# Mixers for one token tile and then for three, in a block of HGRN2, dilated attention and an expert layer

## The chip, the core and the metric

The kernel runs on one core of a Trainium2 chip. The metric is device microseconds of one execution. An engine takes its instructions one after the other, in the order in which the built program has them: TensorE (PE, with its weight loads as PEld), VectorE (DVE), ScalarE (ACT), GpSimd (POOL) and SyncE (SP, which only issues transfers).

## The reference, cut to what matters

512 tokens of width 1024 pass one layer. Everything is float32 outside, and comes out in float32.

```
h = RMSNorm(x);  [q,f,i,og | q,k,v | gate_a | gate_b] = h @ W_in
y_a = HGRN2(q,f,i,og)              # 4 heads, state 128x128 carried over chunks of 64 tokens
y_b = three dilated causal windows, one softmax
x   = x + (sigmoid(gate_a) * (y_a @ W_a) + sigmoid(gate_b) * (y_b @ W_b)) @ W_out
h2  = RMSNorm(x)
q   = h2 @ W_q;  per token and head: the top 16 of 128 x 128 key pairs  (8 heads -> 128 experts of 16384)
x   = x + sum over the 128 pairs of  gelu(u[e] . h2) * gate * v[e]
```

The tokens lie in four tiles of 128 (tile 0 to tile 3). A tile's state depends on the tiles before it, so tiles are mixed in order; the expert layer of a tile needs that tile alone.

## The kernel before, in words

**Mixers.** `Front` (L144) does the mixers of one half of the tokens, and the queries of their expert layer. It is called twice, for tiles 0 and 1 (L716), then for tiles 2 and 3 (L756). Each call streams all dense weights, 37 slots of 256 columns, in tiles `w` of four row blocks (`slot`, L180). The first half is "split": weights and activations are cut into a high and a low float32r half (`halves`, L93: ACT writes the high half, DVE or POOL the low one), and each product is done as three matmuls with 256 moving columns. The second half takes plain float32 matmuls, which the trace shows as two instructions each.

**Routing.** `routing` (L532) picks the 128 experts of every token of a tile, mostly on DVE, in many short instructions.

**The expert layer** reaches its rows in two ways. *Gathered*: for tiles 0 and 3 `u_steps` (L622) lets POOL gather one row of u per token, 128 times (`row`, L616, 512 KB a time), and a DVE pass (L626) takes its dot product with h2; `v_steps` (L637) does the same with v for tile 3 (pass L645). *Streamed*: `hidden` (L783) multiplies all of u, in 128 blocks, with h2 of tiles 1 and 2 (24 matmuls a block), and the last loop (L817) multiplies all of v, block by block, with the weights of tiles 1, 2 and 0 (18 matmuls a block, L834). The weights of a block come from `scatter_steps` (L659): for four tokens at a time DVE makes one-hot rows `e` (L666) and products `eg` (L670), PE multiplies them (L680), ACT stores the result, and it goes to DRAM as `g_d`, from which the last loop loads `Gc`. A block's product begins with the DVE multiplication L825.

**The order.** A scheduler puts each engine's instructions in an order when the program is built. The code guides it: `Pump` (L690) puts steps of gathering and scattering between other work, `ROWS_P` allows 99 gathered rows ahead of the second half's last norm, and L807 holds all but the other tile's gathered rows back:

```
807    with tc.issue_after(last_e2[0].ins):
808        rows(4)
```

Here the u rows of tile 3 are put behind the scatter step's last `eg`; the v rows are added behind them.

Of the kernel before, what the change touches and what calls it, by code (L numbers as in the profile page):

```python
# [22 lines left out]
HALF = 256  # L23
NT = HALF // P
# [13 lines left out]
# Token tiles by how the expert layer reaches them: rows of u gathered, u streamed whole, v streamed whole.  # L38
# VD starts with UD; the tile that is not in it gathers its rows of v.
# [4 lines left out]
NV = len(VD) * P  # L44
GT = 16
NGT = NV // GT
GB = 8
# the first weights' low halves are Pool's
LPOOL = 4
# steps of gathering and scattering before the end of the second half's mixers  # L50
ROWS_P, SCAT_PP = 99, 5
# blocks of hidden values ahead of the products with v, and places for them
NPRE, RING = 46, 58
# tokens in a group of the scatter, groups in flight; groups whose third part ACT scales
GS, EGB = 4, 2
ACT3 = {1: (0, 4, 8, 12), 0: (0, 4, 8, 12), 2: (0, 8)}
ROWS_F, ROWS_D, SCAT_F = 3, 2.0, 0.4
UK, WBUFS, ATB = 4, 4, 3

# columns of the packed per-partition parameters  # L60
C_G1, C_HGN, C_LB, C_QG, C_KG, C_END = 0, 8, 9, 17, 18, 19
# columns of the packed shape constants
M_ATT, M_HG, M_END = 0, 512, 640
# slots of the packed dense weights
# [4 lines left out]
def kernel(ctx: ExitStack, tc: tile.TileContext, x, wst, par, cst, cols, g2, keys, u, v, ut, vr, out):  # L69
# [9 lines left out]
    nc.scalar.activation(root, eps[:, 0:1], AF.Sqrt)  # L79
    h2g = {}  # L80
    hH = const.tile([P, KC, NU], F32R, name="hH")
    hL = const.tile([P, KC, NU], F32R, name="hL")

    fctx = ExitStack()
    wp = fctx.enter_context(tc.tile_pool(name="wp", bufs=WBUFS, side="right"))
    hp = fctx.enter_context(tc.tile_pool(name="hp", bufs=1, side="right"))
# [3 lines left out]
    psb = fctx.enter_context(tc.tile_pool(name="psb", bufs=2, space=PSUM, side="right"))  # L90
# [7 lines left out]
    def accumulate(out, ws, xs, cut, w_stays):  # L98
        """Sum over the blocks of w x, in three products where they come in two parts."""
        ops = []  # L100
        for k, w in enumerate(ws):
            if isinstance(w, tuple):
                x = xs[0][:, k], xs[1][:, k]
                ops += [(w[0], x[0]), (w[0], x[1]), (w[1], x[0])]
            else:
                ops.append((w, xs[:, k]))
        for i, (w, x) in enumerate(ops):
            l, r = (w[:, cut], x) if w_stays else (x[:, cut], w)
            nc.tensor.matmul(out, l, r, start=(i == 0), stop=(i == len(ops) - 1))  # L109
# [10 lines left out]
    reset = fp.tile([P, HALF], F32, name="reset")  # L120
# [3 lines left out]
    # lower bound: softmax over the two logit rows, row 0  # L124
# [5 lines left out]
    # values of the first group by token; of the other two with every fourth token's in a row  # L130
# [13 lines left out]
    class Front:  # L144
        """The mixers of one half of the tokens, and the queries of their expert layer."""

        def __init__(self, h, hi_pool, after_unit):
            self.h, self.hi_pool, self.after_unit = h, hi_pool, after_unit
            split = self.split = hi_pool is not None
            self.units = 0  # L150
            hT = hp.tile([P, KC, HALF], F32R if split else F32, name="hT")
            g1 = par_sb[:, C_G1:C_G1 + KC]
            for t in range(NT):
                xn = sp.tile([P, D], F32, name="sc")
                nc.sync.dma_start(out=xn, in_=x[h * HALF + t * P:h * HALF + (t + 1) * P])
# [3 lines left out]
                for c in range(0, KC, 4):  # L159
# [4 lines left out]
                    if split:  # L164
                        xg = sp.tile([P, 4, P], F32, name="pT")
                        nc.vector.tensor_mul(xg, pt, gain)
                        # the high half lies where h2 of the streamed tokens comes later
                        halves(hH[:, c:c + 4, tk], hT[:, c:c + 4, tk], xg)
                    else:
                        nc.vector.tensor_mul(hT[:, c:c + 4, tk], pt, gain)  # L170
            self.hT = (hH, hT) if split else hT
# [8 lines left out]
        def slot(self, i, ks=slice(0, KC)):  # L180
            """Row blocks ks of a slot's weights, UK of them in a tile: the blocks' operands in order."""
            ops = []
            for k0 in range(ks.start, ks.stop, UK):
                n = min(UK, ks.stop - k0)
                w = wp.tile([P, UK, 256], F32, name="w")
                load = nc.sync.dma_start(out=w[:, :n], in_=wst[i][:, k0 * 256:(k0 + n) * 256].rearrange("p (k c) -> p k c", k=n))
                self.after_unit(load)
                if self.split:
                    w = halves(self.hi_pool.tile([P, UK, 256], F32R, name="wh")[:, :n],
                               self.hi_pool.tile([P, UK, 256], F32R, name="wl")[:, :n], w[:, :n],  # L190
                               nc.gpsimd if self.units < LPOOL or self.units % 4 == 0 else nc.vector)
                self.units += 1
                ops += [tuple(a[:, k] for a in w) if self.split else w[:, k] for k in range(n)]
            return ops

        def proj(self, i, x, T):
            """A slot's 256 columns of the half's products with x, on the partitions (T) or along them."""
            w = self.slot(i)
            pt = psb.tile([P, 2, 256], F32, name="pp")
            for j in range(2):  # L200
                accumulate(pt[:, j], w, x, slice(j * P, (j + 1) * P), T)
            return pt

        def proj_T(self, i):
            return self.proj(i, self.hT, True)

        def proj_N(self, i):
            return self.proj(i, self.hT, False)

        def proj_hgrn(self):  # L210
            pa = hp.tile([P, 2, HG_HEADS, HALF], F32, name="pairA")
            pb = hp.tile([P, 2, HG_HEADS, HALF], F32, name="pairB")
            sq, kk, lf, G2 = pa[:, 0], pa[:, 1], pb[:, 0], pb[:, 1]
            vs = hp.tile([P, 2, NT, 512], F32, name="vs")
            self.vt, self.sil = vs[:, 0], vs[:, 1]
            for b in range(2):
                pt = self.proj_T(W_IN + b)
                nc.scalar.activation(sq[:, 2 * b:2 * b + 2], pt, AF.Sigmoid)
            for b in range(2):
                pt = self.proj_T(W_IN + 2 + b)  # L220
                nc.scalar.activation(lf[:, 2 * b:2 * b + 2], pt, AF.Sigmoid)
# [5 lines left out]
            shp = [P, HG_HEADS, HALF // CH, CH]  # L227
            G = G2.rearrange("p h (c s) -> p h c s", s=CH)
            for hd in range(HG_HEADS):
                nc.vector.tensor_tensor_scan(G2[:, hd], reset, lf[:, hd], 0.0, op0=ALU.mult, op1=ALU.add)  # L230
            eG = hp.tile(shp, F32, name="eG", tag="yaT")
            self.dec = sp.tile([P, HG_HEADS, HALF // CH], F32, name="dec")
            nc.scalar.activation(eG, G, AF.Exp)
            nc.vector.tensor_copy(self.dec, eG[:, :, :, CH - 1])
            nc.vector.tensor_tensor(out=lf.rearrange("p h (c s) -> p h c s", s=CH),
                                    in0=G[:, :, :, CH - 1:CH].to_broadcast(shp), in1=G, op=ALU.subtract)
            nc.scalar.activation(lf, lf, AF.Exp)
            nc.scalar.activation(G2, G2, AF.Exp, scale=-1.0)
            nc.vector.tensor_mul(sq, sq, eG.rearrange("p h c s -> p h (c s)"))
# [3 lines left out]
            for b in range(2):  # L243
                pt = self.proj_N(W_IN + 4 + b)
                nc.scalar.activation(self.vt[:, :, b * 256:(b + 1) * 256], pt, AF.Copy)
            for b in range(2):
                pt = self.proj_N(W_IN + 6 + b)
                o = self.sil[:, :, b * 256:(b + 1) * 256]
                nc.scalar.activation(o, pt, AF.Sigmoid)
                nc.vector.tensor_mul(o, pt, o)  # L250
            self.yaT = hp.tile([P, HG_HEADS, HALF], F32R if self.split else F32, name="yaT", tag="yaT")
            if self.split:
                self.yaT = self.yaT, self.hi_pool.tile([P, HG_HEADS, HALF], F32R, name="yaL", bufs=1)
# [56 lines left out]
        def proj_attn(self):  # L310
            h = self.h
            qgain, kgain = par_sb[:, C_QG:C_QG + 1], par_sb[:, C_KG:C_KG + 1]
            for b in range(3):
                pt = self.proj_N(W_IN + 14 + b).rearrange("p t (n e) -> p t n e", e=64)
                if b == 0:
                    nc.scalar.activation(va[:, h * NT:(h + 1) * NT], pt, AF.Copy)
                    continue
# [476 lines left out]
    with tc.tile_pool(name="php", bufs=2, space=PSUM, side="right") as php, \  # L794
# [6 lines left out]
        for b in range(NPRE):  # L801
            hidden(b, php)
# [100 lines left out]
```

## Time and profile before

| what | us |
|---|---|
| runs: median (lowest to highest of 3) | 1849.44 (1844.27 to 1850.57) |
| profiled execution: span | 1845.0 |
| PE busy | 1674.0 (91%) |
| DVE busy | 1444.1 (78%) |
| ACT busy | 795.6 (43%) |
| POOL busy | 793.6 (43%) |
| read from HBM, written | 443.85 MB, 28.84 MB |

The span of the profile is the time from the first to the last instruction of one execution; the runs have 4.4 us more in the median. A busy share is a mean over stages that have different limits, so a stage is read by itself: the mixers of the first half (0 to 285 us), those of the second (285 to 704), routing, scattering and the first blocks of hidden values (704 to 1055), and the loop of block products (1055 to 1845).

### The profile page before, as it was taken

What the parts mean: (1) busy time and instruction counts of PE and PEld (TensorE: products, weight loads), DVE (VectorE), ACT (ScalarE), POOL (GpSimd) and SP (SyncE); (2) the same over time, 40 slices, a digit from 0 to 9 for tenths busy, and PEclk for the clock granted to TensorE, in tenths of its full rate; (3) what the DMA queues carried; (4) which work ended last, traced back from release to release, by engine and by line L of the source; (5) the groups of instructions that cost most, each with busy time, mean ns of one, the idle gap of its engine ahead of it and who ended that gap; (6) DMA issues with size and microseconds to landing.
All of it is one profiled execution on the core that took longest, in us unless ns stands there. A gap on an engine that the chain in (4) does not pass through costs nothing.

```text
span 1845.0 us, 28370 instructions
## 1 busy us (share of the span) xinstructions
PE 1674.0 (91%) x10573; PEld 1482.8 (80%) x10573; DVE 1444.1 (78%) x2681; ACT 795.6 (43%) x1348; POOL 793.6 (43%) x546
## 2 busy tenths in 40 slices
PE   6999889889789989888867899999999999999987
PEld 6998888667667878777867878888888888888766
DVE  5644547887887758999999977877877788888777
ACT  5655551211114556368756534343343434343232
POOL 3211312463664335556566543344323464444442
PEclk9999999988899989889978899999999999999999
DMA  6453553778787887534455799999988999999887
GB/s 196 153 158 119 175 194 118 270 235 276 244 279 264 297 298 261 183 111 145 152 183 202 238 372 334 339 328 326 367 298 299 345 339 341 340 340 317 288 309 278
DMA packets 169963, 475.61 MB, mean 258 GB/s; under 512 B 14304, under 2 KB 62688, under 8 KB 168800
## 3 DMA queue, kind: packets, MB, share of 16 engines
q1 hardware_dynamic: 112416, 270.56, 43.0%
q0 software_dynamic: 55296, 201.35, 30.9%
q10 hardware_dynamic: 2112, 1.88, 0.3%
q8 instruction: 83, 1.36, 0.3%
q14 instruction: 56, 0.46, 0.1%
HBM read 443.85 MB, written 28.84 MB: 256 GB/s over the span
## 4 chain that ended last, share of the span: by engine, by line
PE 47%; DVE 25%; DMA 11%; issue 9%; POOL 5%; ACT 1%; DVEq 0%; POOLq 0%; SPq 0%; ACTq 0%
PE acc L834 19%; PE pp L109 13%; PE ph L109 10%; DMA row<-in_u_dram,idx 6%; DVE row L626 4%; DVE e L666 4%; DVE eg L670 3%; POOL row L618 3%; DMA Gc<-g_d 3%; PE pg L680 2%; PE pr L680 1%; DVE cs L564 1%; DVE rest L515 1%; DVE ti L514 1%; DVE h2g L645 1%
## 5 line engine op out<-in xcount | busy, mean ns | idle before, releaser
L618 POOL DMA_INDIRECT row<-in_u_dram,idx x206 | 254.9, 1237 | 383.8 <-DVE row L626 274.3
L626 DVE SCALAR_TENSOR_TENSOR row<-row,h2g 128x1024 f32<-128x1024 f32 x206 | 272.4, 1328 | 62.2 <-DMA row<-in_u_dram,idx 61.3
L109 PE MATMUL ph<-hH,uh 128*128 128x256 f32 x1024 | 302.1, 295 | 7.1 <-ACT pre L792 6.0
L109 PE MATMUL ph<-hH,ul 128*128 128x256 f32 x1024 | 302.9, 296 | 5.0 <-POOL ul L95 5.0
L109 PE MATMUL ph<-hL,uh 128*128 128x256 f32 x1024 | 299.0, 292 | 0.0
L834 PE MATMUL acc<-vl,ah 128*128 128x512 f32 x768 | 241.8, 396 | 9.3 <-DVE vl L95 9.3
L834 PE MATMUL acc<-vh,al 128*128 128x512 f32 x768 | 240.0, 393 | 0.0
L94 ACT ACTIVATE uh<-ub 128x1024 fp32r<-128x1024 f32 x128 | 136.7, 1068 | 230.7 <-PE ph L109 214.1
L834 PE MATMUL acc<-vh,ah 128*128 128x512 f32 x768 | 222.5, 395 | 9.9 <-ACT vh L94 9.9
L109 PEld LDWEIGHTS ph<-hH,uh 128*128 128x128 f32 x1024 | 205.9, 201 | 12.8 <-ACT pre L792 7.8
L109 PEld LDWEIGHTS ph<-hH,ul 128*128 128x128 f32 x1024 | 205.5, 201 | 6.3 <-POOL ul L95 5.8
L109 PEld LDWEIGHTS ph<-hL,uh 128*128 128x128 f32 x1024 | 204.6, 200 | 3.8
L680 PEld LDWEIGHTS <-e 128*128 128x128 bf16 x1152 | 124.8, 119 | 73.4 <-DVE eg L670 65.4
L834 PEld LDWEIGHTS acc<-vl,ah 128*128 128x128 f32 x768 | 143.2, 190 | 40.0 <-DVE vl L95 11.8
L834 PEld LDWEIGHTS acc<-vh,ah 128*128 128x128 f32 x768 | 142.9, 190 | 38.2 <-ACT vh L94 10.5
L834 PEld LDWEIGHTS acc<-vh,al 128*128 128x128 f32 x768 | 145.5, 190 | 31.8
L94 ACT ACTIVATE ah<-Gc 128x384 fp32r<-128x384 f32 x128 | 66.9, 523 | 229.4 <-PE acc L834 226.7
L95 DVE TENSOR_TENSOR vl<-vb,vh 128x1024 fp32r<-128x1024 f32 x128 | 156.1, 1219 | 12.2 <-ACT vh L94 12.0
L618 POOL DMA_INDIRECT row<-in_v_dram,idx x76 | 111.6, 1469 | 120.0 <-DVE h2g L645 109.2
L680 PE MATMUL pg<-eg,e 128*128 128x128 bf16 x768 | 103.1, 297 | 51.8 <-DVE eg L670 51.3
L94 ACT ACTIVATE vh<-vb 128x1024 fp32r<-128x1024 f32 x128 | 135.6, 1059 | 28.6 <-DMA vb<-in_vr_dram 27.9
L674 ACT ACTIVATE eg<-e,pk 128x128 bf16<-128x128 bf16 x320 | 115.4, 565 | 70.9 <-DVE e L666 68.1
(279 smaller groups left out, 3582.4 us busy)
## 6 DMA issues: line engine op xcount, KB each, us to landing
w<-in_wst_dram SPq DMA_DIRECT2D x140, 512.0 KB
ub<-in_ut_dram SPq DMA_DIRECT2D x128, 512.0 KB
vb<-in_vr_dram SPq DMA_DIRECT2D x128, 512.0 KB
Gc<-g_d SPq DMA_DIRECT2D x15, 1536.0 KB
g_d<-Gx SPq DMA_DIRECT2D x16, 960.0 KB
g_d<-Gx SPq DMA_DIRECT2D x8, 1024.0 KB
row<-in_u_dram,idx POOLq DMA_INDIRECT x206
sc<-in_x_dram SPq DMA_DIRECT2D x4, 512.0 KB
```

Of the source, the lines that this page charges most:

```text
L94: nc.scalar.activation(hi, x, AF.Copy)
L95: (eng or nc.vector).tensor_tensor(out=lo, in0=x, in1=hi.bitcast(F32), op=ALU.subtract)
L109: nc.tensor.matmul(out, l, r, start=(i == 0), stop=(i == len(ops) - 1))
L514: nc.vector.max_index(out=ids[:, 0:8], in_max=vals[:, 0:8], in_values=src)
L515: nc.vector.match_replace(out=rest[:, :w], in_to_replace=vals[:, 0:8], in_values=src, imm_value=-BIG)
L618: nc.gpsimd.indirect_dma_start(out=r, out_offset=None, in_=src, in_offset=bass.IndirectOffsetOnAxis(ap=index, axis=0))
L626: nc.vector.scalar_tensor_tensor(r, r, 1.0, h2g[T], op0=ALU.mult, op1=ALU.mult, accum_out=hid[:, g, j:j + 1])
L666: nc.vector.tensor_tensor(out=e12, in0=iota[:, None].to_broadcast([P, 2, NKEY, GS]), in1=e[:, 0:2].to_broadcast([P, 2, NKEY, GS]), op=ALU. ...
L670: last_e2[0] = nc.vector.tensor_tensor(out=eg[:, :n], in0=e12[:, 1:2].to_broadcast([P, n, NKEY, GS]), in1=e[:, 2:2 + n].to_broadcast([P, n ...
L674: nc.scalar.activation(eg[:, 2, :, q], e12[:, 1, :, q], AF.Copy, scale=pk3[:, VD.index(T), i + k + q:i + k + q + 1])
L680: nc.tensor.matmul(pt[:, q], e12[:, 0, :, q0 + q], eg[:, j, :, q0 + q], start=(j == 0), stop=(j == 2))
L834: nc.tensor.matmul(acc[t][c], lt, r[:, c * 512:(c + 1) * 512], start=(b == 0 and i == 0), stop=(b == NKEY - 1 and i == 2))
```

## The change

`Front` now takes a list of tiles: first tile 0 alone, with plain float32 matmuls of 128 moving columns, then tiles 1 to 3, split, with 384 moving columns (or 256 where the tokens are the stationary side). Tile 0 is no longer scattered. Its 128 weights are summed per expert on DVE (`same`, 128 passes of 128 elements) and each sum is written by POOL as 128 single words to `w_d` in DRAM, in eight groups of 16 writes, each group behind the one before it (`spread_steps`). The last loop loads `Wc` from there beside `Gc`. The gathering of tile 0's rows and these word writes are spread over the second call's weight loads (`ROWS_F`, `SPREAD_F`). Gathered rows have four places in place of three (before, tile 3's had two more). The routing of tiles 1 to 3 and the scatter steps of tiles 1 and 2 stand between the first 50 blocks of hidden values; the order rule of L807 is gone.

```diff
-UK, WBUFS, ATB = 4, 4, 3
+ROWS_F, SPREAD_F = 2.4, 3.6
+NPRE, RING = 50, 56
+LDVE = 3
+ROUTE1, ROUTE2, SCAT_H = 6, 22, 2
+ROWS_H, ROWS_D = 0.8, 1.8
+UK, WBUFS, WSBUFS, ATB = 4, 2, 4, 2
...
+    def spread_steps():
+        for j in range(P):
+            same = rt.tile([P, P], F32, name="same")
+            nc.vector.scalar_tensor_tensor(same, fulls, fulls[:, j:j + 1], hid[:, 0], op0=ALU.is_equal, op1=ALU.mult,
+                                           accum_out=wsum[:, j:j + 1])
+            d = nc.gpsimd.indirect_dma_start(out=w_d.rearrange("i j t -> (i j t)")[:, None], in_=wsum[:, j:j + 1],
+                                             out_offset=bass.IndirectOffsetOnAxis(ap=place[:, j:j + 1], axis=0),
+                                             in_offset=None)
...
+            if j % TOPK == 0:
+                before, spread[:] = list(spread), []
+            behind(d, before)
...
+    f = Front(UG[:1], False, lambda load: None)
...
+    f = Front(tuple(range(1, 4)), True, background)
...
     routing(0, rq0)
-    rows.add(u_steps(0))
...
+    rows.add(u_steps(UG[0]))
+    rows.add(spread_steps())
+    mixers(f)
...
-                     nc.gpsimd if b < NPRE else nc.vector)
+                     nc.gpsimd if b < NPRE and b % LDVE else nc.vector)
...
-        routing(2, rq2)
-        scat.add(scatter_steps(0, pg_bank))
-        scat.add(scatter_steps(2, pg_bank))
-        scat(P)
-        for b in range(NPRE):
-            hidden(b, php)
-        routing(3, rq3)
...
-    rows.add(u_steps(3))
-    with tc.issue_after(last_e2[0].ins):
-        rows(4)
+        routing(3, rq3)
+        rows.add(u_steps(3))
+        for b in range(NPRE):
+            if b == ROUTE1:
+                routing(1, rq1)
+                scat.add(scatter_steps(1, pg_bank))
+            if b == ROUTE2:
+                routing(2, rq2)
+                scat.add(scatter_steps(2, pg_bank))
+            hidden(b, php)
+            rows(ROWS_H)
+            if b % SCAT_H == 0:
+                scat(1)
+        scat(P)
     rows.add(v_steps(3))
```

What this makes of the engines' orders is seen at three places.

**DVE, among the last scatter steps, before.** `e` and `eg` are the scatter step's tiles, `row` and `rq` hold gathered rows of u for tile 3, the rest is routing of tile 3.

```order
L585 TENSOR_REDUCE idf<-sel 128x16
L516 MAX tv<-rest 128x8
L670 TENSOR_TENSOR eg<-e_7475,pk 128x1024
L588 CAST idx<-idf 128x16
L517 MAX_INDEX ti<-tv,rest 128x8
L666 TENSOR_TENSOR e_7497<-iota,pk 128x1024
L515 MATCH_REPLACE rest<-tv,ssb 128x128
L626 SCALAR_TENSOR_TENSOR rq,hid<-rq,h2g 128x1024
L666 TENSOR_TENSOR e_7515<-iota,pk 128x1024
L670 TENSOR_TENSOR eg<-e_7497,pk 128x1536
```

One row pass stands here among two scatter groups. In all, 148 row passes, all of u, stand ahead of the first L825, and 96 scatter groups.

**DVE, among the last scatter steps, in the change.** L718 and L722 make `e` and `eg`; L673 is the row pass with v of tile 3; L658 is the row pass with u.

```order
L722 TENSOR_TENSOR eg<-e_9313,pk 128x1024
L718 TENSOR_TENSOR e_9335<-iota,pk 128x1024
L673 SCALAR_TENSOR_TENSOR h2g<-rowx,hid,h2g 128x1024
L722 TENSOR_TENSOR eg<-e_9335,pk 128x1024
L718 TENSOR_TENSOR e_9357<-iota,pk 128x1024
L673 SCALAR_TENSOR_TENSOR h2g<-rowx,hid,h2g 128x1024
L722 TENSOR_TENSOR eg<-e_9357,pk 128x1536
L718 TENSOR_TENSOR e_9447<-iota,pk 128x1024
L673 SCALAR_TENSOR_TENSOR h2g<-rowx,hid,h2g 128x1024
L722 TENSOR_TENSOR eg<-e_9447,pk 128x1024
```

Each group now has a pass with a row of v beside it. In all, 256 passes with u and 72 with v stand ahead of the first L888 (the block multiplication that was L825), and 64 scatter groups. The low halves `ul` of u's blocks that DVE makes ahead of it are 26, where they were 5.

**POOL, from the last gathered rows of tile 0 to the end of the second call's mixers, in the change.** L650 gathers a row, L697 writes 128 words, `wl` is the low half of half a weight tile (two row blocks), L482 adds the two branches.

```order
L650 DMA row<-in_u_dram,idx 128x1024
L697 DMA w_d<-wsum,place 2097152x1 x4
L100 TENSOR_TENSOR wl<-w,wh 128x512
L697 DMA w_d<-wsum,place 2097152x1 x11
L100 TENSOR_TENSOR wl<-w,wh 128x512
L697 DMA w_d<-wsum,place 2097152x1
L482 TENSOR_TENSOR pairA<-pairA,pairB 128x768 x3
L100 TENSOR_TENSOR wl<-w,wh 128x512
L697 DMA w_d<-wsum,place 2097152x1 x13
L482 TENSOR_TENSOR pairA<-pairA,pairB 128x768
L697 DMA w_d<-wsum,place 2097152x1 x17
L100 TENSOR_TENSOR wl<-w,wh 128x512
```

POOL makes every third `wl` (48 of 144), and from the first word write on the last 12 of them stand between 128 word writes. Before, there were no word writes, and the second call's weights were not split.

## Rows read from the trace of the kernel before

**Rows 1.** Busy time of each engine in the four stages, with clock and DMA.

```profile
core 0: us, PE busy (x) PEld busy (x) DVE busy (x) ACT busy (x) POOL busy (x), PEclk, DMA share, GB/s
0.00:285.00 285.00, 258.48 (x2246) 245.83 (x2247) 145.31 (x216) 150.13 (x247) 63.89 (x32) 0.98 0.51 162
285.00:704.00 419.00, 372.95 (x2037) 309.05 (x2036) 330.07 (x917) 129.54 (x281) 189.47 (x154) 0.92 0.76 257
704.00:1055.00 351.00, 283.87 (x2119) 268.51 (x2117) 336.85 (x737) 222.74 (x410) 213.50 (x128) 0.88 0.54 180
1055.00:1845.00 790.00, 758.70 (x4176) 659.37 (x4176) 631.86 (x813) 293.21 (x412) 326.71 (x234) 0.98 0.92 327
```

**Rows 2.** What VectorE waited for, 285 to 704, then 704 to 1055 us.

```profile
DVE row L626 <- DMA row<-in_u_dram,idx: 53.3, 38, 5.2
...
DVE e L666 <- PE pg L680: 6.6, 8, 1.6
DVE row L626 <- DMA row<-in_u_dram,idx: 2.8, 2, 1.6
```

**Rows 3.** Pieces of the chain that ended last: start, us, what, instructions.

```profile
621.71 5.61 PE pp L109 x26
627.32 2.85 PE pr L680 x24
...
1163.42 2.84 PE ph L109 x24
...
1579.40 4.14 PE acc L834 x18
```

**Rows 4.** VectorE groups by form: shapes, count, busy us, mean ns, idle before.

```profile
L626 DVE SCALAR_TENSOR_TENSOR row<-row,h2g 128x1024 f32<-128x1024 f32 x206 | 272.4, 1328 | 62.2 <-DMA row<-in_u_dram,idx 61.3 <-issue 0.7
L666 DVE TENSOR_TENSOR e<-iota,pk 128x1024 bf16<-128x1024 bf16 x96 | 103.8, 1089 | 27.5 <-PE pr L680 20.7 <-PE pg L680 6.6
L95 DVE TENSOR_TENSOR ul<-ub,uh 128x1024 fp32r<-128x1024 f32 x82 | 101.1, 1233 | 53.7 <-ACT uh L94 51.6 <-ACT ah L94 1.2 <-issue 0.7
L645 DVE SCALAR_TENSOR_TENSOR h2g<-row,hid,h2g 128x1024 f32<-128x1024 f32 x76 | 97.3, 1280 | 0.5
L670 DVE TENSOR_TENSOR eg<-e,pk 128x1024 bf16<-128x1024 bf16 x80 | 74.5, 940 | 0.1
L670 DVE TENSOR_TENSOR eg<-e,pk 128x1536 bf16<-128x1536 bf16 x16 | 28.7, 1796 | 0.0
L626 DVE DVE_READ_ACCUMULATOR row<-row,h2g 128x1 f32 x206 | 16.5, 80 | 0.0
L297 DVE SCALAR_TENSOR_TENSOR ks<-pt,ss,vs 128x128 f32<-128x128 f32 x16 | 4.5, 342 | 0.1
```

**Rows 5.** First and last row passes, their gathers and the block multiplication, by line.

```profile
L618 POOL DMA_INDIRECT row<-in_u_dram,idx x206: 932/1008/2000, 314.0 to 1429.1; - x103
L626 DVE SCALAR_TENSOR_TENSOR row<-row,h2g x206: 1171/1218/3326, 320.5 to 1437.1; 128x1024 f32<-128x1024 f32 x103
...
L825 DVE TENSOR_TENSOR Gc<-pre,Gc x128: 405/417/428, 1054.8 to 1775.7; 128x256 f32<-128x256 f32 x128
```

**Rows 6.** All projections (L109) on PE in the first stage.

```profile
0.00:285.00 285.00, 220.91 (x1728) 211.94 (x1728) 0.98 0.51 162
```

**Rows 7.** 320 to 560 us: the row passes (two instructions each), then all engines.

```profile
320.00:560.00 240.00, 107.61 (x152) 0.89 0.78 259
...
320.00:560.00 240.00, 205.20 (x1077) 164.02 (x1077) 198.97 (x582) 45.59 (x97) 129.12 (x104) 0.89 0.78 259
```

**Rows 8.** First stage: low and high halves (L95) on DVE and POOL.

```profile
0.00:285.00 285.00, 83.45 (x68) 54.93 (x22) 0.98 0.51 162
```

**Rows 9.** POOL's groups: a gathered row, a low half of a weight tile.

```profile
L618 POOL DMA_INDIRECT row<-in_u_dram,idx x206 | 254.9, 1237 | 383.8 <-DVE row L626 274.3 <-DVE ti L517 16.8 <-DVE tv L516 16.8
L95 POOL TENSOR_TENSOR wl<-w,wh 128x1024 fp32r<-128x1024 f32 x21 | 53.6, 2558 | 193.0 <-ACT wh L94 141.6 <-PE pp L109 14.5 <-PE pt L402 13.6
```

More of the change, by code (lines that the diff above doesn't have):

```diff
@@ L178, in rstd, with slot @@
             return st[:, 1:2]
-        def slot(self, i, ks=slice(0, KC)):
-            ops = []
+        def slot(self, i, ks):
+            src = lambda k, n: wst[i][:, k * 256:(k + n) * 256].rearrange("p (k c) -> p k c", k=n)
             for k0 in range(ks.start, ks.stop, UK):
                 n = min(UK, ks.stop - k0)
-                w = wp.tile([P, UK, 256], F32, name="w")
[L186 to L208, printed above, removed]
+                if not self.split and k0 % (2 * UK):
+                    for j in range(0, n, 2):
+                        w = wsp.tile([P, 2, 256], F32, name="wl" if j else "wh")
+                        nc.sync.dma_start(out=w, in_=src(k0 + j, 2))
+                        yield k0 + j - ks.start, [w[:, k] for k in range(2)]
+                    continue
@@ new lines, in slot @@
+                w = wp.tile([P, UK, 256], F32, name="w")
+                self.after_unit(nc.sync.dma_start(out=w[:, :n], in_=src(k0, n)))
+                if not self.split:
+                    yield k0 - ks.start, [w[:, k] for k in range(n)]
+                    continue
+                for j in range(0, n, 2):
+                    h = halves(wsp.tile([P, 2, 256], F32R, name="wh"), wsp.tile([P, 2, 256], F32R, name="wl"), w[:, j:j + 2],
+                               nc.gpsimd if self.units % LPOOL == 0 else nc.vector)
+                    self.units += 1
+                    yield k0 + j - ks.start, [tuple(a[:, k] for a in h) for k in range(2)]
@@ new lines, in products @@
+        def products(self, i, ks, x, outs, w_stays):
+            last = ks.stop - ks.start - 1
+            units = []
+            for k0, ws in self.slot(i, ks):
+                units.append((k0, ws))
+                for out, cut, alone in outs:
+                    if alone:
+                        accumulate(out, ws, x, cut, w_stays, k0, last)
+            for out, cut, alone in outs:
+                for k0, ws in units if not alone else ():
+                    accumulate(out, ws, x, cut, w_stays, k0, last)
@@ L751, in background @@
+    place = rt.tile([P, P], I32, name="place")
+    wsum = rt.tile([P, P], F32, name="wsum")
+    pr = rctx.enter_context(tc.tile_pool(name="pr", bufs=1, space=PSUM, side="left"))
+    row_places = [(rq_pool, "rq")] * 3 + [(gat, "row")]
     def background(load):
         with tc.issue_after(load.ins):
-            rows(min(ROWS_F / 2, ROWS_P - rows.done))
-        scat(min(SCAT_F / 2, SCAT_PP - scat.done))
-    f = Front(1, None, background)
-    routing(0, rq0)
-    rows.add(u_steps(0))
-    f.proj_hgrn()
@@ L770 @@
+    nc.gpsimd.memset(zero, 0.0)
+    for k in range(0, NKEY, 32):
+        nc.scalar.dma_start(out=w_d[:, k:k + 32].rearrange("p (a b) t -> p a (b t)", b=4),
+                            in_=zero[:, None].to_broadcast([P, 8, 512]))
+    routing(0, rq0)
+    rows.add(u_steps(UG[0]))
+    rows.add(spread_steps())
+    mixers(f)
+    rows(P - rows.done)
+    rq1, rq2, rq3 = f.post()
     with tc.issue_after(f.last_h2.ins):
         rows(2 * P)
-        scat(P)
+    hH, hL = f.hu
     fctx.close()
```

414 lines of the change are left out of this document (212 added, 202 removed).

## The prediction, made before the changed kernel was run

> **What bounds the kernel now.** I read the busy time by stage first [rows 1]. Read as one number, PE at 91% would be the bound. By stage it is so only at both ends. In the first 285 us PE is busy for 258 and DVE for 145; in the loop of block products, from 1055 us, PE is busy for 759 of 790 and DVE for 632. In between it is DVE's turn: 337 of 351 us from 704 to 1055, while PE has 284 at a lower granted clock. DVE's own waits say the same: from 704 on its two longest sum to 9.4 us; between 285 and 704 it waits for gathered rows (53.3 us) and loses 89 in all [rows 1, 2].
>
> So the time is two sums. The first block product needs the scattered weights, and L825 stands on DVE behind whatever the scheduler put ahead of it. Up to there the time is DVE's work plus DVE's idle time: 145 + 330 + 337 = 812 of work, and 140 + 89 + 14 = 243 idle, makes 1055 [rows 1], where L825 begins [rows 5]. Behind it PE sets the pace, for 790 us. The sum is made against this execution's span of 1845.0; the runs' median lies 4.4 us higher, which I add at the end.
>
> **Term 1, DVE's work ahead of the first product.** The orders above give the counts, the groups' busy time divided by their counts gives the prices [rows 4].
> - Row passes with u: 256 in place of 148, 108 x 1.32 = +143.
> - Row passes with v: 72 in place of none, 72 x 1.28 = +92. These 180 passes were beside the block products before; the rule that held them behind the last `eg` is gone.
> - Scatter groups: 64 in place of 96, 32 x (1.08 + 0.93) = -64; eight more third parts go to ACT, 8 x (1.79 - 0.93) = -7.
> - The sums per expert: 128 passes of 128 elements. Nearest is L297 with 0.28 busy, and the accumulator's 0.08: 128 x 0.36 = +46 (36 without the read; 54 with the full 0.342).
> - Low halves of u's blocks: 26 in place of 5, 21 x 1.23 = +26.
>
> The low halves of the weights (96 half-size ones for 52) and the mixers' elementwise work are the same elements cut differently: nothing. Together +236: 1048 us of DVE work must be done before the first product can begin. No wait has to be guessed for that.
>
> **Term 2, DVE's idle time ahead of it, by stage.**
>
> *Tile 0 alone.* PE does 352 float32 matmuls of 128 columns, two instructions each. A 128-column instruction takes 2.85 / 24 = 0.119 in the trace and one of 256 float32 columns 5.61 / 26 = 0.216 [rows 3], so 704 x 0.119 = 84 and 224 x 0.216 = 48. Work other than projections was 258 - 221 = 38 for two tiles [rows 1, 6], 19 for one. With the 26 us in which PE was not busy before: 177; one tile hides its own chains less well, 0 to 40 more, I take 18: 195. DVE's work in it is half of 145 less the split's 83 [rows 8], 31: idle 164 (before 140).
>
> The Trainium skill's page TensorE: Matmul & The Clock Gate (Back-to-back issue gap) gives about 81 ns for a sustained weight load and matmul at 128 columns. By that the 704 instructions would take 57 and the total 27 us less; the trace disagrees with its 119 ns, which I use.
>
> *Tile 0's rows.* The first row pass came 36 us behind the first mixers [rows 5]; I take 40, as the norms of three tiles stand there too. Then 128 passes. Before, 76 passes took 240 us, 3.16 each, with three places, so a place turned over in 9.5 us [rows 7]. Four places would give 2.37; no gain 3.16. I take 2.6, nearer to the four places, because DVE, 83% busy there, now has the split's low halves as well: 333 us. DVE idle was 17%; for 373 us I take 13%, 48.
>
> *Word writes.* This is the new wait. From the first word write on, the last 12 `wl` of POOL stand between 128 writes in its queue, and PE needs one of them for every three half weight tiles. Behind a write on POOL thus wait `wl`, PE and the rest of the mixers, and from there h2, the routing of three tiles and all blocks of u. No write of this kind is in the trace. A gather also addresses 128 rows, so its duration is the nearest: median 1.01 (0.93 to 2.00) [rows 5]; 129. Twelve half-size `wl` at 2.56 / 2 [rows 9]: 15. Seven times a group waits until the one before has landed, 0 to 6.5 us (a gather's time from issue to its pass, 314.0 to 320.5 [rows 5]); I take 3: 21. With 6 for the gelu ahead: 171 us. PE alone would need 75: 36 half tiles are 9 slots of 48 instructions of 384 columns, at 0.173 (midway between 2.84 / 24 for 256 and 4.14 / 18 for 512 columns [rows 3]). DVE has the sums' 46 in it and some 40 of low halves, merging and norm: idle 85.
>
> The Trainium skill's page DMA: Bandwidth & Descriptors (Anatomy of one DMA) gives a transfer from GpSimd a fixed 2 us, most of it the receipt of the write. By that the seven waits would be 14, the sum 7 less. No run here shows it yet.
>
> *Routing, scatter, first blocks.* What is left of the 1048 is 1048 - 31 - 325 - 86 = 606. DVE lost 4% in this stage before [rows 1]: 24 more. POOL has 200 gathers at 1.24 [rows 9] and 33 low halves in these 630 us; it fits, but a row that comes late now stops DVE with all behind it.
>
> First product: 195 + 373 + 171 + 630 = 1369, or 1048 of work and 164 + 48 + 85 + 24 = 321 idle. Before: 1055.
>
> **Term 3, the block products.** PE has 59 blocks of u done ahead, before 52: 7 x 2.84 = -20. It was not busy for 31 us; with 180 rows fewer to gather in here, some of that goes: 0 to 20, I take 10. The extra high and low halves for `Wc` lie beside PE, on engines with room: DVE loses 235 us of row passes. 790 - 30 = 760. The end: 1369 + 760 = 2129, and 4 for the median: **2133 us**.
>
> **Rivals.**
> - *The word writes hold nobody up* (POOL issues them in a fraction of a gather's time). Then PE's 75 stand for the 171: 2037. For: 512 bytes instead of 512 KB. Against: both address 128 rows. 15%.
> - *The word writes are dear.* At 2.00 us (the longest gather) and 6.5 a wait the stage takes 323: 2285. The Trainium skill's page DMA: Bandwidth & Descriptors (Specifications) says that below 512 B a transfer is a read, a change and a write; here that would mean longer waits between the groups, and no run shows it yet. For: these are writes of single words. Against: a write does not wait for the one just before it. 10%.
> - *The other side: PE, not DVE, sets the first product.* The added passes would then fill DVE's idle time. PE's work there: 150 (tile 0), 302 + 57 (three tiles: 1056 x 0.173 + 1008 x 0.118, and three times 19), 59 x 2.84 = 168, 64 groups x 12 x 0.119 = 91, routing 30: 798; with 42 not busy, 840 + 760 = 1600. It decides, and the change is faster, once the first product begins before 1845 - 760 = 1085. For: PE's total falls. Against: DVE's work alone is 1048, and tile 0's 164 idle stand on top: 1212. Only an order on the chip that is not the one shown could do it. 4%.
>
> **How the numbers follow.** My case, with all terms within their bounds, has 71%. With every low bound at once (177, 2.37, 0.93 and no waits, no idle behind) it gives 2015, with every high one (215, 3.16, 2.00 and 6.5, 10% idle) some 2420; half of each side is enough for 8 in 10, and with the first two rivals the range is 1980 to 2290. Runs of this kernel tell 0.3% (5 us) from no change. Slower by more has 95%, from the first three cases and a little of the last; faster 4%, the last; within 0.3% 1%.
>
> **What would show it.** In the changed profile the first L888 should come near 1370, with 256 passes of L658 and 72 of L673 ahead of it; the stage ahead of it should show DVE over 90% busy and PE at a lower granted clock. Tile 0's mixers should end near 195. Between the last gather of tile 0 and the routing of tile 3, POOL should be the one that PE's `wl` waits for, over some 170 us. The products should take 760. The prediction is wrong in its main term if L888 comes before 1212, and in its second if PE waits for nothing on POOL there.

## The result, and the profile after the change

The changed kernel takes **2141.02 us** (median of 4 runs, 2140.38 to 2151.73); the kernel before, run beside it, 1848.74 (1844.27 to 1850.57). The ratio is 1.160, with a 95% interval of 1.157 to 1.163: 16% slower. The forecast was 2133, within 1980 to 2290. The profiled execution took 2141.4 us with a span of 2139.3 and a mean granted clock of 0.865.

The first view answers to [rows 1]: busy time of each engine of the changed kernel, cut where tile 0's mixers end, where the word writes begin, where h2 of the three tiles is there, and at the first block product.

```profile
core 0: us, PE busy (x) PEld busy (x) DVE busy (x) ACT busy (x) POOL busy (x), PEclk, DMA share, GB/s
0.00:180.00 180.00, 159.68 (x1217) 145.59 (x1218) 43.83 (x127) 58.65 (x151) 6.21 (x13) 0.99 0.76 246
180.00:569.00 389.00, 330.61 (x2239) 295.80 (x2238) 335.94 (x744) 142.69 (x283) 242.91 (x179) 0.89 0.79 268
569.00:710.60 141.60, 68.42 (x389) 64.92 (x388) 70.94 (x222) 26.12 (x56) 104.29 (x99) 0.69 0.22 62
710.60:1381.30 670.70, 376.15 (x2451) 345.11 (x2449) 619.41 (x1357) 252.48 (x472) 477.10 (x346) 0.71 0.70 234
1381.30:2139.00 757.70, 732.64 (x4008) 639.09 (x4008) 428.78 (x644) 291.36 (x525) 74.45 (x53) 0.99 0.64 212
```

PE still sets the pace of the last stage (733 of 758 us) and DVE that of the one before it (619 of 671). The last stage is 32 us shorter than it was; the 294 us come from what lies ahead of it: 1381.3 in place of 1054.8 [rows 5]. DVE is busy for 1070.1 us up to there and idle for 311.2; before it was 812 and 243 [rows 1].

The next rows are of the same kernel, by line; they answer to [rows 5]. Each tells duration (shortest, median, longest, in ns) and the first and last start: passes with u over tile 0's places and over the last tile's, passes with v, the word writes, the block multiplication.

```profile
L658 DVE SCALAR_TENSOR_TENSOR rq<-rq,h2g x96: 1172/1218/3120, 222.0 to 561.6; 128x1024 f32<-128x1024 f32 x96
...
L658 DVE SCALAR_TENSOR_TENSOR rowx<-rowx,h2g x96: 1197/1212/3619, 786.0 to 1202.2; 128x1024 f32<-128x1024 f32 x96
...
L673 DVE SCALAR_TENSOR_TENSOR h2g<-rowx,hid,h2g x95: 1261/1281/2840, 1207.7 to 1563.5; 128x1024 f32<-128x1024 f32 x95
...
L697 POOL DMA_INDIRECT w_d<-wsum,place x128: 965/969/1428, 569.8 to 772.9; - x128
...
L888 DVE TENSOR_TENSOR Gc<-pre,Gc x128: 417/421/427, 1381.3 to 2055.1; 128x256 f32<-128x256 f32 x128
```

All of the last tile's passes with u and the first of those with v lie between 786 and 1381, ahead of L888, as the order said. Two places show who waits for what stands ahead in a queue. In the second half of the three tiles' mixers PE's waits, 569 to 710.6 us, are led by POOL:

```profile
PE pp L113 <- POOL wl L100: 42.8, 4, 17.6
PE pp L113 <- ACT hT L99: 8.9, 2, 7.7
PE pp L113 <- DVE xl L100: 7.9, 2, 5.3
```

The longest of the four, in order of time (start, duration, what, idle time before it): 13 word writes go through POOL, 1.27 us from one to the next, and only then the low halves that PE stands for.

```profile
655.12 0.97 POOL L697 DMA_INDIRECT w_d<-wsum,place  x1 [0.31 <-issue]
656.39 0.97 POOL L697 DMA_INDIRECT w_d<-wsum,place  x1 [0.30 <-issue]
...
670.39 0.97 POOL L697 DMA_INDIRECT w_d<-wsum,place  x1 [0.30 <-issue]
671.38 2.49 POOL L100 TENSOR_TENSOR wl<-w,wh 128x512 fp32r<-128x512 f32 x2
...
672.70 0.58 PE L113 MATMUL pp<-wl,hT 128*128 128x256 f32 x1 [17.56 <-POOL wl L100]
```

The other place is the routing of tile 2. Its indices are split by L634 on DVE, at 1272.4, behind the last passes with u (to 1204.7) and 29 passes of L673 with v (from 1207.7); PE waits for it:

```profile
1272.72 0.47 PE L637 MATMUL pr<-ident,ssb 128*128 128x128 f32 x1 [92.09 <-DVE ssb L634]
```

For PE these 92 us are lost; on DVE they are work. DVE was busy for 80 of them, and 64 of the 80 went to passes that the first product does not need.

### The profile page after: what moved, and what is told of

Read it like the earlier page. It is cut to its first block, busy times and chain, and to the rows that moved or that the text cites. A ratio compares the mean times of both kernels' runs of the same rounds, so it can differ in the third digit from the quotient of the medians.

```text
span 2139.3 us, 28780 instructions
## 1 busy us (share of the span) xinstructions
PE 1667.5 (78%) x10298; PEld 1490.5 (70%) x10298; DVE 1498.9 (70%) x3087; ACT 771.3 (36%) x1485; POOL 905.0 (42%) x688
## 4 chain that ended last, share of the span: by engine, by line
PE 46%; DVE 24%; DMA 13%; POOL 8%; issue 7%; ACT 1%; ACTq 0%; DVEq 0%; POOLq 0%; SPq 0%
PE acc L898 24%; PE ph L113 11%; PE pp L113 9%; DMA w<-in_wst_dram 4%; DVE rowx L658 4%; POOL w_d L697 2%; DVE row L658 2%; DMA rowx<-in_u_dram,idx 2%; DVE same L695 2%; DVE wl L100 2%; DMA row<-in_v_dram,idx 1%; DMA rq<-in_u_dram,idx 1%; POOL rowx L650 1%; DVE h2g L673 1%; DVE rq L658 1%
## 5 line engine op out<-in xcount | busy, mean ns | idle before, releaser
L113 PE MATMUL ph<-hH,uh 128*128 128x256 f32 x1024 | 313.2, 306 | 38.2 <-ACT uh L99 23.5
L113 PEld LDWEIGHTS ph<-hH,ul 128*128 128x128 f32 x1024 | 217.0, 213 | 74.1 <-DVE ul L100 45.4
L113 PEld LDWEIGHTS ph<-hL,uh 128*128 128x128 f32 x1024 | 216.7, 212 | 2.8
L100 DVE TENSOR_TENSOR ul<-ub,uh 128x1024 fp32r<-128x1024 f32 x95 | 120.9, 1272 | 107.9 <-ACT uh L99 107.8
L650 POOL DMA_INDIRECT rowx<-in_v_dram,idx x96 | 129.4, 1347 | 134.2 <-DVE h2g L673 112.2
L99 ACT ACTIVATE wh<-w 128x512 fp32r<-128x512 f32 x144 | 87.5, 627 | 212.6 <-DMA w<-in_wst_dram 104.4
L650 POOL DMA_INDIRECT rowx<-in_u_dram,idx x96 | 126.0, 1312 | 76.8 <-DVE rowx L658 28.8
L697 POOL DMA_INDIRECT w_d<-wsum,place x128 | 128.1, 1001 | 64.1 <-DVE same L695 28.0
L650 POOL DMA_INDIRECT rq<-in_u_dram,idx x96 | 124.7, 1299 | 69.1 <-DVE rq L658 34.7
L113 PE MATMUL pp<-wl,hT 128*128 128x256 f32 x376 | 113.3, 328 | 51.8 <-POOL wl L100 39.3
```

Source lines behind the costliest of these rows:

```text
L99: nc.scalar.activation(hi, x, AF.Copy)
L100: (eng or nc.vector).tensor_tensor(out=lo, in0=x, in1=hi.bitcast(F32), op=ALU.subtract)
L113: nc.tensor.matmul(out, l, r, start=(k == 0 and i == 0), stop=(k == last and i == len(ops) - 1))
L650: nc.gpsimd.indirect_dma_start(out=r, out_offset=None, in_=src, in_offset=bass.IndirectOffsetOnAxis(ap=index, axis=0))
L697: d = nc.gpsimd.indirect_dma_start(out=w_d.rearrange("i j t -> (i j t)")[:, None], in_=wsum[:, j:j + 1], out_offset=bass.IndirectOffsetOnA ...
```

## The experiments

Eight kernels were run, each timed beside the kernel before. Theory: the time is DVE's work in its order up to the first product, plus DVE's idle time up to there, plus 758 us of products. Each run that only moves work tests whether the sum holds.

### The hold put back

```
+                last_e2[0] = nc.vector.tensor_tensor(out=eg[:, :n], ...
...
     rows.add(v_steps(3))
+    with tc.issue_after(last_e2[0].ins):
+        rows(4)
```

> The changed kernel with the hold of the kernel before put back: the pump's next rows may be gathered only behind the last eg. In DVE's order 173 passes with u and none with v stand ahead of the first block product, where the changed kernel has 256 and 73; the other 156 come beside the products. Theory (DVE's work in its order sets the first product): 83 x 1.32 + 73 x 1.28 = 203 us less, first product at 1381 - 203 = 1178, and the products again about 760 to 790, as DVE has 429 + 203 = 632 us in them: 1940 to 1975 in all. Rival (the passes only filled time in which the scattered weights were late anyway): the first product stays within 40 us of 1381 and the time within 30 of 2141 or, with slower products, above it.

Measured: 1975.77 us (1972.58 to 1981.25), ratio to the kernel before 1.069 [1.066, 1.072]. By stage, from the start of the word writes, then from h2 of the three tiles to the first product, then the products:

```profile
566.90:713.50 146.60, 70.17 (x388) 63.86 (x388) 68.64 (x219) 25.73 (x55) 105.05 (x99) 0.70 0.23 68
713.50:1206.90 493.40, 357.64 (x2451) 334.66 (x2449) 419.72 (x1115) 244.60 (x471) 268.33 (x189) 0.81 0.45 149
1206.90:1972.00 765.10, 734.44 (x4008) 639.41 (x4008) 605.42 (x885) 292.18 (x526) 293.09 (x210) 0.98 0.90 317
```

The first product comes at 1206.9, 174 us earlier. DVE's work up to there fell from 1070.1 to 868.3, by 202 where 203 was expected; its idle time rose from 311 to 339. That the work agrees so closely is partly chance: the passes taken away had cost 223 us, and the other instructions ahead of the first product now took 21 more. What is late next is PE: DVE now waits 32 us for the banks in which PE multiplies the scatter groups, 2.8 in the changed kernel:

```profile
DVE e L720 <- PE pg L734: 32.3, 30, 4.9
```

The 156 passes cost next to nothing beside the products: 765 us for 758, with DVE busy for 605 of them. The rival, that the passes only filled idle time, is out.

### A larger dose

```
-ROWS_H, ROWS_D = 0.8, 1.8
+ROWS_H, ROWS_D = 0.8, 2.1
...
-        rows.add(u_steps(3))
...
-            rows(ROWS_H)
...
+    rows.add(u_steps(3))
+    with tc.issue_after(last_e2[0].ins):
+        rows(4)
     rows.add(v_steps(3))
```

> A larger dose of the same: all of the last tile's rows with u are held as well. Ahead of the first product stand 132 passes with u and none with v, 41 fewer than in the run before; but 46 passes with v come behind the last product. Theory: first product 41 x 1.32 = 54 us earlier than with the smaller dose, near 1124, and 46 x 1.28 = 59 us behind the end of the products, so that the total is within 20 us of the smaller dose's. Rival (DVE has stopped to be the bound ahead of the products): the first product comes less than 25 us earlier than with the smaller dose, and the total is 35 us or more above it.

Measured: 1959.29 us (1956.93 to 1968.22), ratio 1.061 [1.058, 1.064]. The last two stages:

```profile
714.40:1137.90 423.50, 343.64 (x2451) 323.46 (x2449) 351.29 (x1033) 243.85 (x471) 215.17 (x148) 0.87 0.37 123
1137.90:1956.40 818.50, 735.92 (x4008) 640.49 (x4008) 652.68 (x967) 292.13 (x526) 355.68 (x251) 0.95 0.92 323
```

The first product comes 69 us earlier, not 54; work fell by 69 and idle time stayed, 339 us. The passes taken away had been dear: in the smaller dose the 45 passes of this stage took 82.7 us, 1.84 each (the last section shows why). The 46 passes behind the last product took 53, so 16 of the 69 are left. DVE is still the bound.

### No low halves between the word writes

```
-                               nc.gpsimd if self.units % LPOOL == 0 else nc.vector)
+                               nc.gpsimd if self.units % LPOOL == 0 and rows.done < P else nc.vector)
```

> The smaller dose (the hold put back), and from the end of tile 0's rows on all low halves of the weights are VectorE's, so that none stands between the word writes in POOL's queue. Passes ahead of the first product as in the smaller dose: 173. Theory (PE's wait for wl behind the word writes is what stretches the second half of the three tiles' mixers): PE loses no time to POOL there, which was 65 us, DVE gets 12 x 0.66 = 8 more: h2 of the three tiles comes 45 to 60 us earlier and so does the end, 1885 to 1925 if the smaller dose takes 1940 to 1975. Rival (the three tiles are bound by DVE's sums and elementwise work or by the weights' loads there): within 15 us of the smaller dose.

Measured: 1982.23 us (1974.78 to 1987.15), ratio 1.072 [1.069, 1.076], which overlaps the interval of the hold alone. The theory fell: 45 to 60 us were expected. The two stages around h2:

```profile
566.50:691.20 124.70, 73.79 (x393) 66.26 (x392) 64.80 (x222) 26.02 (x56) 87.57 (x82) 0.71 0.28 81
691.20:1210.50 519.30, 362.44 (x2451) 338.70 (x2449) 420.60 (x1125) 242.96 (x471) 273.01 (x194) 0.80 0.43 141
```

PE no longer waits for POOL in the mixers, and they end 22 us earlier; the next stage gets 26 us longer with the same work on DVE (420.6 for 419.7). The writes end at 807 here, at 777 with the hold alone. It may be that the low halves were only the ones that stood nearest behind the writes; that is not shown. The trace of this run names no releaser for the waits that are left between 640 and 670 us; what holds PE there stays open.

### No word writes

```
-            d = nc.gpsimd.indirect_dma_start(out=w_d.rearrange("i j t -> (i j t)")[:, None], ...
...
-            spread.append(d)
```

> The smaller dose with the 128 word writes left out: tile 0's weights never reach the block products; the sums per expert on VectorE stay. Theory: the same gain as with the low halves on VectorE, 45 to 60 us, and at most 20 more, because the writes cost through what stands behind them in POOL's queue and not through memory. Rival (the writes hold up more than the low halves, by the gathers and the products of routing that follow them in POOL's queue): 80 to 130 us below the smaller dose. Second rival (the writes hold nothing up): within 15 us of it.

Measured: 1886.48 us (1884.45 to 1894.23), ratio 1.021 [1.018, 1.024].

```profile
565.00:636.10 71.10, 56.66 (x406) 53.82 (x405) 66.30 (x218) 28.46 (x59) 19.32 (x12) 0.95 0.44 141
636.10:1116.20 480.10, 363.09 (x2451) 339.40 (x2449) 410.22 (x1123) 243.61 (x471) 226.01 (x148) 0.81 0.46 153
```

The writes cost 89 us: the rest of the mixers takes 71 us in place of 147, and the stage behind is 13 shorter. By its number the first rival, 80 to 130, holds. Its reason, the gathers and the routing that follow the writes, fits only the 13 us behind h2; the other 75 lie in the mixers. DVE's idle time up to the first product is 262 us, against 339.

### Half the word writes

```
+            if j >= P // 2:
+                yield 1
+                continue
             d = nc.gpsimd.indirect_dma_start(...
```

> The hold put back, and only the first 64 of the 128 word writes are issued: half of tile 0's weights never reach the block products; the sums per expert on VectorE all stay. Without any write the time was 89 us less than with all. Theory (each write costs its 1.27 us of POOL's queue, so 128 of them 163, of which rather more than half is waited for): half the writes give back half, 35 to 55 us, so 1920 to 1940. Rival (the cost is a fixed one, a late start or a last landing before the products): less than 20 us, 1956 or more. Second rival (the mixers are past the point of being held by 64 writes): nearly all, 75 or more, 1901 or less.

Measured: 1949.72 us (1947.51 to 1959.19), ratio 1.056 [1.051, 1.060]. None of the three bands holds it: half the writes give back 26 us, so the first 64 cost 63 (1949.72 against 1886.48) and the other 64 cost 26. h2 of the three tiles comes at 636, 694 and 713.5 us with 0, 64 and 128 writes. So a write has no single price. That the price depends on what still stands behind the write would explain it, and is not shown.

### The word writes beside the first blocks

```
-            else:
-                rows(SPREAD_F)
...
-    rows.add(spread_steps())
...
+    words.add(spread_steps())
...
             rows(ROWS_H)
+            words(2.7)
```

> The hold put back, and the 128 sums with their word writes come beside the first blocks of u, 2.7 for each block, not beside the three tiles' mixers. Theory (the writes hold up whoever stands behind them in POOL's queue; beside the first blocks POOL has room, but DVE, which is the bound there, gets the 128 x 0.43 = 55 us of sums): h2 of the three tiles 77 us earlier, as without writes, the first product some 20 earlier, 1935 to 1965. Rival (POOL's 163 us are the cost wherever they stand, as the low halves of u and routing's selections stand behind them there too): first product no earlier or later than with the writes beside the mixers, 1975 to 2030. Second rival (the sums cost nothing beside the first blocks): 1900 or less.

Measured: 1962.22 us (1961.00 to 1964.92), ratio 1.061 [1.058, 1.065]; 14 us below the hold alone.

```profile
563.00:629.10 66.10, 55.29 (x408) 53.14 (x408) 34.63 (x48) 29.41 (x61) 19.98 (x12) 0.96 0.46 148
629.10:1194.60 565.50, 368.02 (x2451) 342.29 (x2449) 446.73 (x1292) 243.57 (x471) 358.81 (x276) 0.77 0.40 130
```

The total lies in the theory's band, but its reason is only half of it. The mixers end 84 us earlier, and the stage behind takes 72 us more, of which only 27 are DVE's work (446.7 for 419.7); 45 are idle time. DVE's waits of that stage say for whom:

```profile
DVE rowx L658 <- DMA rowx<-in_u_dram,idx: 39.6, 16, 7.0
DVE e L720 <- PE pg L734: 30.9, 26, 6.4
DVE idf L612 <- POOL sel L611: 29.8, 9, 10.6
```

The gathers of the last tile's rows and the selections of the routing now stand behind the writes on POOL (2.7 and 4.6 us of such waits with the hold alone). Over the whole way to the first product DVE's idle time is 336 us, the same as the 339 with the writes beside the mixers. The first rival, that POOL's time is the cost wherever it stands, is right for the idle time.

### Three places for tile 0's rows

```
-    row_places = [(rq_pool, "rq")] * 3 + [(gat, "row")]
+    row_places = [(rq_pool, "rq")] * 3
```

> The hold put back, and tile 0's rows have three places, not four (the fourth, row, is left out of the list until the three tiles' mixers end). Passes in each part of DVE's order stay. Theory of the prediction (a place turns over in 9.5 us, so the places set the pace of the rows: 3.16 us a pass with three): the 128 passes take 404 us, not 340, and the whole gets 50 to 65 us longer, 2025 to 2040. Rival (the rows go at the pace of the mixers, whose weight loads release them at 2.4 for each, and the places are never short): under 15 us longer.

Measured: 1981.86 us (1976.92 to 1993.12), ratio 1.074 [1.069, 1.079]: no difference from the hold alone that the intervals can tell.

```profile
L658 DVE SCALAR_TENSOR_TENSOR rq<-rq,h2g x128: 1165/1224/3746, 227.0 to 618.5; 128x1024 f32<-128x1024 f32 x128
```

The places do set the pace: from the first pass to the last 3.08 us each (391.5 / 127), against 2.66 with four. The waits of the two kernels between 220 and 570 us agree, first the hold alone, then three places:

```profile
DVE rq L658 <- DMA rq<-in_u_dram,idx: 24.7, 17, 3.9
```

```profile
DVE rq L658 <- DMA rq<-in_u_dram,idx: 66.3, 42, 3.7
```

But the whole does not get longer. The stage of the rows takes 447 us in place of 387, and the rest of the mixers 82 in place of 147:

```profile
180.00:626.70 446.70, 365.70 (x2359) 325.48 (x2359) 357.99 (x766) 148.04 (x290) 241.09 (x187) 0.87 0.73 239
626.70:708.40 81.70, 39.93 (x265) 38.66 (x265) 47.92 (x196) 17.91 (x43) 63.10 (x62) 0.73 0.28 85
```

While the rows go slower the mixers go on, so fewer of them are left when the writes begin: h2 comes at 708.4, with the hold alone at 713.5.

### What helped, together

The larger dose, the writes beside the first blocks, and five `rowx` places with six rows held (all six places, so that none of the held rows slips ahead).

```
-    rx = ctx.enter_context(tc.tile_pool(name="rx", bufs=3, side="right", **TILE))
+    rx = ctx.enter_context(tc.tile_pool(name="rx", bufs=5, side="right", **TILE))
...
+    with tc.issue_after(last_e2[0].ins):
+        rows(6)
```

> What helped, together: all rows of the last tile held behind the last eg, sums and word writes beside the first blocks of u, and six places for the held rows in place of four, so that 20 passes with v come behind the last product and not 46. Ahead of the first product stand 134 passes with u and none with v. Theory (the first product is DVE's work in its order plus its idle time): against the run with late writes 39 x 1.32 = 51 us less work, and POOL has 39 gathers fewer, so most of the 40 us in which DVE waited there for gathered rows goes too; the first product near 1194 - 51 - 35 = 1108, the products 765, and 20 x 1.28 = 26 behind them: 1885 to 1925. Rival (with the rows gone POOL is the bound, by the 128 writes at 1.27 and the low halves of u): the first product at 1140 or later, 1930 or more. It is not expected to beat the kernel before: tile 0 alone with VectorE idle for 136 us and 55 us of sums stay.

Measured: 1919.09 us (1918.18 to 1920.82), ratio 1.039 [1.036, 1.042].

```profile
628.10:1134.70 506.60, 360.21 (x2454) 336.81 (x2454) 382.29 (x1213) 243.99 (x471) 309.64 (x238) 0.81 0.33 108
1134.70:1917.50 782.80, 739.47 (x4008) 640.68 (x4008) 649.04 (x963) 294.28 (x526) 341.73 (x248) 0.98 0.93 335
```

The time is in the theory's band, the first product between the two: 60 us earlier than with late writes, where 86 were forecast. Work fell by 64 and idle time rose by 4: the 40 us of late rows are gone, and the routing waits for POOL's selections twice as long.

```profile
DVE idf L612 <- POOL sel L611: 60.6, 9, 15.9
```

It is 222 us faster than the changed kernel and 73 slower than the kernel before; no version was faster than the kernel before.

The runs in one table, up to the first product (DVE busy and idle from their stages, us):

| kernel | DVE work | DVE idle | first product | products and tail | span |
|---|---|---|---|---|---|
| before | 812 | 243 | 1055 | 790 | 1845.0 |
| changed | 1070 | 311 | 1381 | 758 | 2139.3 |
| hold put back | 868 | 339 | 1207 | 765 | 1972.0 |
| larger dose | 799 | 339 | 1138 | 819 | 1956.4 |
| hold, no `wl` between the writes | 864 | 347 | 1211 | 766 | 1976.4 |
| hold, no writes | 854 | 262 | 1116 | 768 | 1884.5 |
| hold, half the writes | 857 | 324 | 1182 | 766 | 1948.1 |
| hold, late writes | 859 | 336 | 1195 | 766 | 1961.1 |
| hold, three places | 873 | 340 | 1213 | 763 | 1976.3 |
| together | 795 | 340 | 1135 | 783 | 1917.5 |

With all 128 writes and the hold, idle time is 336 to 347 in six orders; without them 262.

## Why the prediction was right, and where its steps were not

**The sum.** First product 1381 for 1369, products 758 for 760. That the total came within 8 us is partly luck: the four stages ahead of the first product were off by -15, +16, -29 and +41 us. By stage, length and DVE idle, forecast and measured:

| stage | forecast | idle | measured | idle |
|---|---|---|---|---|
| tile 0 alone | 195 | 164 | 180 | 136 |
| tile 0's rows | 373 | 48 | 389 | 53 |
| word writes, to h2 | 171 | 85 | 142 | 71 |
| routing, scatter, first blocks | 630 | 24 | 671 | 51 |

**Term 1, the work ahead: shown.** 256 passes with u and 73 with v (72 of L673 and the first, L671) stood ahead, as the order had them; 1070 us of work for 1048. Taking passes away moved the first product by the work removed: in the first dose less 28 us of idle time that came back, in the second by all of it.

The work grew by 258 us, where 236 were forecast, and its parts were further off than the sum: passes with u 167 for 143, with v 104 for 92, the sums per expert 60 for 46, low halves 44 for 26, but scatter groups 105 less for 71 less. The price of a pass was a mean over two places. Before, the 148 passes ahead of the first product took 1.40 us each, the other 108, all beside the products, 1.22; in the change the 256 took 1.46 each. The first two rows are all passes with u ahead of the first product, before and in the change, the third the sums per expert (count of instructions in brackets, two for a pass or a sum):

```profile
0.00:1054.80 1054.80, 207.64 (x296) 0.92 0.62 206
...
0.00:1381.30 1381.30, 374.72 (x512) 0.80 0.69 228
...
0.00:1381.30 1381.30, 59.79 (x256) 0.80 0.69 228
```

These times hold the accumulator's read. It is not a cost beside the pass: with the reads the 256 passes take 374.7 us, without them 373.6. So the 0.08 that the sums' price had for it was not needed; a sum took 0.47 with its read, not 0.36.

**Term 2, tile 0 alone.** 180 for 195: most of the 18 us for chains that a single tile hides less well were not needed, as the sum without them was 177. Its 0.119 us for 128 columns was read from a bf16 product (L680), and nearly carried over to float32: eight such instructions fill 69.85 to 70.75 us of the changed kernel, 0.11 each. The 81 ns of the Trainium skill's page TensorE: Matmul & The Clock Gate (Back-to-back issue gap) would have made it 150, or 168 with the 18.

**Term 2, tile 0's rows.** The passes took 341 us (222.0 to 562.8) for 333, and their pace is that of the places, as three places showed: 3.08 for a forecast of 3.16. But the step built on it, that a slower row is a longer whole, is wrong. Rows and mixers run side by side, and time lost on the rows came back from the stage behind them. Adding the two stages as if each had its own limit gave the right total because their sum was right, not because each is a price.

**Term 2, word writes.** This term was mis-sized in its parts. A write holds POOL's queue for 1.27 us (0.97, and 0.30 until the next), not 1.01. That makes 163 for 129, and the writes lasted 204 us. The waits for the group before were 8.5 us in 5, not 21. POOL also waited 28.0 us for the sums on DVE, and for this wait the forecast had no term:

```profile
POOL w_d L697 <- DVE same L695: 28.0, 32, 10.7
...
POOL w_d L697 <- DMA w_d<-wsum,place: 8.5, 5, 3.8
```

For the waits between groups the Trainium skill's page DMA: Bandwidth & Descriptors (Anatomy of one DMA) gave 14, nearer than the forecast's 21, and the 2.2 us from issue to landing that the trace shows for a write (the median) agrees with its 2. That the mixers would end only with the last write was wrong: h2 came at 710.6, when 41 writes were still to come. The effect came out near all the same: leaving the writes out, with the hold put back, gave back 89 us where the forecast had 171 - 75 = 96. As 13 of the 89 lie behind h2, and the parts were off in both directions, that is partly luck.

**Routing, scatter, first blocks.** DVE over 90% busy (619 of 671) and PE at a granted clock of 0.71 came as described. Idle time was 51 for 24; of it 13 us was one wait right behind the mixers.

**The rivals.** Word writes that hold nobody up: out, by 89 us. Dear ones, with long waits between the groups for single words: out, by 8.5 us in 5 waits. The Trainium skill's page DMA: Bandwidth & Descriptors (Specifications) says that a transfer below 512 B is a read, a change and a write; the trace shows no wait between the groups beyond these 8.5 us. PE as the one that sets the first product: out, by the two doses. It comes into view once the passes are gone, with 32 us of waits for the scatter's banks.

## What to carry to other kernels

Filler work is cheap only where something holds it behind what the bound needs: here the same 156 passes cost 174 us ahead of the first product and 7 beside the products. Find the engine that ends a stage last, and count its work and its idle time up to that point; counted so, one dose of passes came out within 1 us of the work forecast (partly by chance), the other 15 us off, because a pass has not the same price everywhere. When a queue's time is the cost, moving it moves the waits: ask who stands behind it in the new place before expecting a gain.

## What the runs showed of the hardware

A write of 128 single words holds POOL's queue like a gather of 128 rows of 4 KB: 969 ns against medians of 1145 to 1226 (shortest 932), 512 bytes or 512 KB. And VectorE's passes and sums stretch while POOL computes, not while it gathers or writes. A pass with u of 4.39 us in the changed kernel, in order of time, first POOL and then DVE:

```profile
912.86 1.56 POOL L609 TENSOR_TENSOR sel<-eq,ci 128x800 f32<-128x800 bf16 x1
914.37 2.37 POOL L100 TENSOR_TENSOR ul<-ub,uh 128x1024 fp32r<-128x1024 f32 x1
918.11 1.91 POOL L650 DMA_INDIRECT row<-in_u_dram,idx  x1 [1.37 <-DVE tv L540]
```

```profile
913.44 4.39 DVE L658 SCALAR_TENSOR_TENSOR row<-row,h2g 128x1024 f32<-128x1024 f32 x1
...
917.97 1.20 DVE L658 SCALAR_TENSOR_TENSOR rowx<-rowx,h2g 128x1024 f32<-128x1024 f32 x1
```

The pass ends 1.09 us after POOL's second computation; the next pass, beside a gather, takes 1.20 in all. So nearly the whole of the long pass came behind that computation. All long passes of the changed kernel look like this one: 53 of the 383 of L658 and L673 take more than 1.5 us, and in each of the 53 a computation of POOL ends 1.08 to 1.10 us before the pass does. The 283 that no computation of POOL overlaps take 1.32 us at most. Of the passes with u, 173 stand clear of POOL's computations and take 1.21 in the mean; the other 83 take 1.99. This accounts for the 1.46 us of a pass ahead of the first product. In the stage of the smaller dose, where a pass cost 1.84, a computation of POOL stood beside 20 of the 45. At 1.21 the 256 would take some 311 us and not 374: an estimate, as no run took POOL's computations away.

A sum per expert is 0.35 us in its kind, and one took 7.30:

```profile
592.86 5.34 POOL L482 TENSOR_TENSOR pairA<-pairA,pairB 128x768 f32<-128x768 f32 x3
598.16 1.26 POOL L100 TENSOR_TENSOR wl<-w,wh 128x512 fp32r<-128x512 f32 x1
599.59 0.98 POOL L697 DMA_INDIRECT w_d<-wsum,place  x1 [0.17 <-issue]
```

```profile
592.27 7.30 DVE L695 SCALAR_TENSOR_TENSOR same<-fulls,hid 128x128 f32<-128x128 f32 x1
...
599.62 0.35 DVE L695 SCALAR_TENSOR_TENSOR same<-fulls,hid 128x128 f32<-128x128 f32 x1
```

It ends at 599.57, 0.15 us after the last of four POOL computations in a row, and the next sum takes 0.35 again, beside a word write. The Trainium skill's page SBUF — State Buffer (SBUF: two separate sides) says that the two engines share a pair of ports, which one instruction holds to its end while the other is blocked. The trace agrees that DVE waits for the end of a POOL computation. Two things it shows beyond that: DVE was let in only after four of them, and by the profile's records the sum had begun 0.59 us before the first.
